# SBUF pools of a diffusion backbone exchange their places along the partition

## The chip, the cores and the metric

The kernel runs on one core of a Trainium2 chip. The metric is the device time in microseconds of one execution; the number quoted for a kernel is the median of its runs. The profile is of one more execution, taken by the hardware profiler.

## The reference

A backbone of two layers over 512 latent tokens of width 1024 with 256 context tokens in front (batch 1), in float32. Layer 0 mixes with attention (4 differential heads and 8 grouped-query heads), layer 1 with a spatial-gating MLP. Each layer ends with a gated ConvFFN of inner width 2816, and all sub-layers have an adaLN-modulated RMSNorm ahead and a gated residual behind. Cut to what matters here:

```python
for l in range(DEPTH):                       # DEPTH = 2
    h_lat = modulate(rms_norm(x, mix_norm[l]), sh1, sc1)
    y_lat = attention_mixer(...) if l % 2 == 0 else sgu_mixer(...)
    x = x + g1 * y_lat
    x = x + g2 * conv_ffn(modulate(rms_norm(x, ffn_norm[l]), sh2, sc2), ...)
return rms_norm(x, final_norm)

def conv_ffn(h, w_up, conv_w, conv_b, w_down):
    z = h @ w_up                              # 1024 -> 5632
    z = conv_w[0] * z[t-1] + conv_w[1] * z[t] + conv_w[2] * z[t+1] + conv_b
    g, u = jnp.split(z, 2, axis=-1)
    return (jax.nn.silu(g) * u) @ w_down      # 2816 -> 1024
```

## The kernel before

The weights are cut into 182 units of 128x1024 float32 (`N_UNITS`, line 50). `fetch` (line 185) loads a unit by a DMA of SP's queue into one of four `raws` buffers. `ens` (line 286) then splits it into a high part (a cast on ACT, line 292) and a low part (a subtraction on DVE, line 296, through `sub`, line 137), both of type fp32r, each in a tile of its own. A product of two split operands is three matmuls, high by high, high by low, low by high (`mm3`, line 131), so a unit, which holds eight 128x128 blocks, stands for 24 matmuls, each with its own weight load.

The FFN is `ffn` (line 1051). Up projection: 44 units a layer, each one 128-row block of the output; units 0 to 3 run as two halves of 256 columns, where the norm of the tokens is still being finished, and units 4 to 43 with all 512 columns. Down projection (`out_proj`, line 961): 8 output blocks m of 22 k-steps each, so k-step q = 22 m + k takes block q % 8 of unit q // 8, 22 units a layer; m = 0 to 5 with 512 columns, m = 6 and 7 as halves of 256. In both, the weights are the stationary operand; the activations, the moving operand, lie in slots.

Where a split unit goes is decided by `wslot` (line 278). The two FFNs' units go in part to the weight pool `wpool` (`area2`, six tiles of 4 KiB a partition), the rest to `slots` (37 such tiles):

```python
for b, n, per in ((U_UP0, 44, 4), (U_DN0, 22, 8), (U_UP1, 44, 4), (U_DN1, 22, 8)):
    if b <= u < b + n and (u - b) % per < 3:
        return area2.tile([128, 1024], F32R, name=nm(p), tag="W2")
return slot(p)
```

So of four up units the first three lie in the weight pool and the fourth in slots; of eight down units the first three in the weight pool and five in slots. A pool unit has two of the six tiles (high and low), and three units go once round the pool.

The pools stand one behind the other in each partition, in the order in which they are opened (lines 76 to 81). In the compiled program, counted in KiB from the start of the partition: 16 reserved by the compiler and a few constants of its own; `const` to 23.5; `slots` 23.5 to 171.5; `raws` 171.5 to 187.5; `temps` (six buffers of 2 KiB) to 199.5; `tiny` to 199.9; then `att`, eight buffers of 3 KiB for the score tiles of attention and a few tables, 199.9 to 223.9. After attention `att` is closed (line 940) and `wpool`, 24 KiB as well, is opened in the same place (line 943). In each down projection the tiles of its unit 0 start at 199.9 and 219.9, those of unit 1 at 215.9 and 211.9, those of unit 2 at 207.9 and 203.9. The compiler places tiles up to 224 KiB.

In attention, a score tile (`e`, line 651) lies in `att`; `ptrans` (line 657) transposes it 128x128 at a time on TensorE with the score block as the stationary operand and `ident` as the moving one (`tr`, line 128); `build_q` (line 608) does the same with blocks of q from slots. `ones_m` is the stationary operand of the norm sums (`rstd_bc`, line 311), whose moving operand is in temps. `row_mm` (line 352) multiplies the adaLN matrices of layer 0, read from raws as moving operands (tiles `am`).

Of the kernel before, what the change touches and what calls it, by code (L numbers as in the profile page):

```python
# [9 lines left out]
F32 = mybir.dt.float32  # L10
# [43 lines left out]
def hybrid_backbone(  # L54
# [18 lines left out]
    nc = tc.nc  # L73
    V, A, G, T_, SY = nc.vector, nc.scalar, nc.gpsimd, nc.tensor, nc.sync

    const = ctx.enter_context(tc.tile_pool(name="const", bufs=1))
    slots = ctx.enter_context(tc.tile_pool(name="slots", bufs=37))
    raws = ctx.enter_context(tc.tile_pool(name="raws", bufs=4))
    temps = ctx.enter_context(tc.tile_pool(name="temps", bufs=6))
    tiny = ctx.enter_context(tc.tile_pool(name="tiny", bufs=12))  # L80
    area = tc.tile_pool(name="att", bufs=8)
    att = area.__enter__()
    psP = ctx.enter_context(tc.tile_pool(name="psP", bufs=4, space=PSUM))
# [60 lines left out]
    sm = const.tile([128, SM_COLS], F32, name="sm")  # L144
    cw = const.tile([128, 352], F32, name="cw")
    cb = const.tile([128, D], F32, name="cb")
    ident = const.tile([128, 128], F32, name="ident")
    ones_m = const.tile([128, 128], F32, name="ones_m")
    md = const.tile([128, 96], F32, name="md")
    tab1 = att.tile([128, 768], F32, name="tab1", tag="E")  # L150
    tab2 = att.tile([128, 768], F32, name="tab2", tag="E")
# [1170 lines left out]
```

## Time and profile before

| | us |
|---|---|
| median of 3 runs (1290.22 to 1291.27) | 1290.73 |
| the profiled execution | 1293.27 |
| its span, first to last instruction | 1291.5 |
| TensorE busy | 1239.1 (96%) |
| VectorE busy | 757.9 (59%) |
| ScalarE busy | 594.4 (46%) |
| GpSimd busy | 248.1 (19%) |
| the four longest unbroken TensorE pieces of the chain | 709.7 |

Engines are PE (TensorE matmul), PEld (its weight loads), DVE (VectorE), ACT (ScalarE), POOL (GpSimd), SP (SyncE, which issues DMAs). L126 is a line of the kernel; nearly all matmuls stand under L126, the line of `mm`, so they are told apart by what they write: `up` and `op` are the up and down projections, `sc` scores, `pt` transposed scores. Matmuls overlap, so a matmul's own duration is longer than the time from one to the next; that time is had by dividing a stretch by the weight loads that start in it (the x behind PEld).

### The profile page before, as it was taken

To read this page: it belongs to the slowest core of one execution; us is meant where nothing else is said; L and a number is where in the kernel's file an instruction comes from. 1 tells how busy PE (TensorE), PEld (TensorE's weight loads), DVE (VectorE), ACT (ScalarE), POOL (GpSimd) and SP (SyncE) were. 2 spreads that over 40 slices of the span, in tenths; PEclk is the share of its full clock that TensorE was granted. 3 is DMA by queue.
4 is the path that set the end of the run, shared out by engine and by line. 5 is a ranking of instruction groups with operands and counts; after the bars stand their busy time and mean duration, and the time that the engine had idled before them with its cause. 6 is when DMAs were issued, how large, how long until landed. Compare 5 with 4: busy or idle time off the path is not lost.

```text
span 1291.5 us, 17180 instructions
## 1 busy us (share of the span) xinstructions
PE 1239.1 (96%) x6722; PEld 1043.7 (81%) x6722; DVE 757.9 (59%) x1116; ACT 594.4 (46%) x970; POOL 248.1 (19%) x171
## 2 busy tenths in 40 slices
PE   5899999889989999999999999999999999999997
PEld 3688988777769888888888898888988888888887
DVE  4466367688867866666775433455575565655312
ACT  3343355676645665666543134433454444444211
POOL 0102266564540344444600000000000000000001
PEclk9999999999889999999999999999999999999999
DMA  9521434763321455555577404224033232325201
GB/s 371 201 66 37 128 115 147 216 176 99 98 82 34 151 192 196 194 195 179 166 258 246 148 3 145 82 82 147 19 128 99 83 113 82 102 94 163 82 1 66
DMA packets 49505, 167.40 MB, mean 130 GB/s; under 512 B 6144, under 2 KB 6672, under 8 KB 49424
## 3 DMA queue, kind: packets, MB, share of 16 engines
q1 hardware_dynamic: 49424, 166.30, 39.3%
q8 instruction: 53, 0.87, 0.3%
q14 instruction: 28, 0.23, 0.1%
HBM read 152.12 MB, written 2.10 MB: 119 GB/s over the span
## 4 chain that ended last, share of the span: by engine, by line
PE 74%; DVE 3%; ACT 1%; POOL 0%; DMA 0%; issue 0%; DVEq 0%; SPq 0%; ACTq 0%; POOLq 0%
PE up L126 38%; PE op L126 23%; PE su L126 3%; PE sv L126 3%; PE sc L126 1%; PE og L126 1%; PE po L126 1%; DVE osq L758 1%; PE pt L129 1%; PE mx L126 1%; PE pn L126 1%; PE nps L126 1%; DVE mx L650 1%; DVE u L331 0%; DMA kk<-ks 0%
## 5 line engine op out<-in xcount | busy, mean ns | idle before, releaser
L126 PE MATMUL up<-h,wh 128*128 128x512 f32 (+1 forms) x1536 | 447.0, 375 | 0.7 <-DVE h L333 0.6
L126 PEld LDWEIGHTS up<-h,wh 128*128 128x128 f32 x1536 | 280.4, 188 | 57.0 <-DVE h L333 1.0
L137 DVE TENSOR_TENSOR wl<-wr,wh 128x1024 fp32r<-128x1024 f32 x176 | 224.2, 1283 | 166.5 <-ACT wh L292 144.2
L126 PE MATMUL up<-h,wl 128*128 128x512 f32 (+1 forms) x768 | 286.2, 375 | 0.0
L292 ACT CAST wh<-wr 128x1024 fp32r<-128x1024 f32 x182 | 188.4, 1048 | 122.3 <-PE up L126 48.0
L126 PE MATMUL op<-p,wh 128*128 128x512 f32 (+1 forms) x880 | 227.5, 348 | 0.0
L126 PEld LDWEIGHTS op<-p,wh 128*128 128x128 f32 x880 | 154.0, 189 | 22.0
L126 PEld LDWEIGHTS up<-h,wl 128*128 128x128 f32 x768 | 144.6, 188 | 27.5
L126 PE MATMUL op<-p,wl 128*128 128x512 f32 (+1 forms) x440 | 153.0, 348 | 0.0
L252 POOL TENSOR_TENSOR ar<-ar,cb 128x1024 f32<-128x1024 f32 x40 | 98.8, 2485 | 155.9 <-DMA ar<-in_adaT_dram 110.3
L1210 POOL TENSOR_TENSOR of<-of,rstd 128x512 f32<-128x512 f32 x2 | 3.6, 1797 | 641.2 <-ACT rstd L318 641.2
L1063 DVE SCALAR_TENSOR_TENSOR z<-up,cw,z 128x511 f32<-128x511 f32 x88 | 65.4, 745 | 52.3 <-ACT z L1062 52.3
L126 PEld LDWEIGHTS op<-p,wl 128*128 128x128 f32 x440 | 83.1, 189 | 10.9
L1062 ACT ACTIVATE z<-up,cw 128x512 f32<-128x512 f32 x88 | 68.0, 774 | 21.2 <-PE up L126 21.2
L953 DVE SCALAR_TENSOR_TENSOR x<-op,md,x 128x512 f32<-128x512 f32 (+1 forms) x42 | 25.9, 622 | 87.8 <-PE op L126 87.7
L650 DVE TENSOR_REDUCE mx<-sc 128x1 f32<-128x768 f32 x64 | 60.8, 951 | 22.7 <-PE sc L126 14.7
L652 ACT ACTIVATE e<-sc,mx 128x768 f32<-128x768 f32 x64 | 57.9, 905 | 32.5 <-DVE mx L650 30.0
L1065 DVE SCALAR_TENSOR_TENSOR z<-up,cw,z 128x511 f32<-128x511 f32 x88 | 65.7, 749 | 2.7
L1068 ACT ACTIVATE z<-z 128x512 f32<-128x512 f32 x44 | 27.8, 632 | 84.7 <-DVE z L1065 84.7
L126 PE MATMUL sc<-kk,qs 128*128 128x512 f32 (+1 forms) x256 | 58.3, 349 | 7.2 <-DMA kk<-ks 6.5
L326 ACT ACTIVATE sq<-x 128x512 f32<-128x512 f32 (+1 forms) x37 | 20.4, 559 | 84.8 <-DVE x L953 84.2
L142 ACT CAST p<-z 128x512 fp32r<-128x512 f32 x44 | 27.3, 619 | 69.3 <-DVE z L1069 69.3
(206 smaller groups left out, 1879.5 us busy)
## 6 DMA issues: line engine op xcount, KB each, us to landing
wr<-in_W_dram SPq DMA_DIRECT2D x182, 512.0 KB, 3.8
ar<-in_adaT_dram SPq DMA_DIRECT2D x56, 512.0 KB, 4.5
am<-in_adaM_dram SPq DMA_DIRECT2D x24, 512.0 KB, 3.9
ar<-in_adaN_dram SPq DMA_DIRECT2D x16, 512.0 KB, 8.6
kk<-ks SPq DMA_DIRECT2D x20, 256.0 KB, 4.2
x<-in_xT_dram SPq DMA_DIRECT2D x8, 512.0 KB, 5.2
kk<-ks SPq DMA_DIRECT2D x20, 128.0 KB, 3.3
qs<-qh SPq DMA_DIRECT2D x16, 128.0 KB, 2.4
```

The costliest lines, as they stand in the source:

```text
L126: pe(T_.matmul(out=o, lhsT=l, rhs=r, start=st, stop=sp))
L137: return V.tensor_tensor(out=o, in0=a, in1=b, op=ALU.subtract)
L142: return A.copy(out=hi, in_=src), sub(lo, src, f(hi))
L252: return (G.tensor_tensor(out=tl, in0=tl, in1=cv, op=ALU.mult), A.activation(out=temp("aj", 1024, BF16), in_=tl, func=AF.Identity, accum_o ...
L292: last["hi"] = A.copy(out=hi, in_=r)
L650: V.tensor_reduce(out=m, in_=ps[:, 0:768], axis=AX.X, op=ALU.max, negate=True)
L652: A.activation(out=e, in_=ps[:, 0:768], func=AF.Exp, bias=m, scale=1.0, accum_out=sm_out)
L953: last["x"] = V.scalar_tensor_tensor(out=xv, in0=ps, scalar=md[:, gcol + m:gcol + m + 1], in1=xv, op0=ALU.mult, op1=ALU.add)
L1062: A.activation(out=t, in_=p, func=AF.Identity, bias=cw[:, cv + 3:cv + 4], scale=cw[:, cv + 1:cv + 2])
L1063: V.scalar_tensor_tensor(out=t[:, 1:512], in0=p[:, 0:511], scalar=cw[:, cv:cv + 1], in1=t[:, 1:512], op0=ALU.mult, op1=ALU.add)
L1065: V.scalar_tensor_tensor(out=t[:, 0:511], in0=p[:, 1:512], scalar=cw[:, cv + 2:cv + 3], in1=t[:, 0:511], op0=ALU.mult, op1=ALU.add)
L1068: last_silu[0] = A.activation(out=z[0], in_=z[0], func=AF.Silu)
```

## The change

`const`, `raws`, `temps` and `tiny` are opened from the right, that is from the upper end of the space downward; `slots` and `att` (and with it `wpool`, which takes its place) stay on the left. `ident` and `ones_m` move from `const` to a new pool `mats` at the very beginning of the left side. Sizes, buffer counts, loops and the order in the program are as before. Added up from the sizes, in KiB: `mats` 16.1 to 17.1, `slots` 17.1 to 165.1, `att` and later `wpool` 165.1 to 189.1; from the upper end, `const` 217.6 to 224, `raws` 201.6 to 217.6, `temps` 189.6 to 201.6, `tiny` below that.

```diff
@@ -73,11 +73,12 @@
     nc = tc.nc
     V, A, G, T_, SY = nc.vector, nc.scalar, nc.gpsimd, nc.tensor, nc.sync
 
-    const = ctx.enter_context(tc.tile_pool(name="const", bufs=1))
+    const = ctx.enter_context(tc.tile_pool(name="const", bufs=1, side="right"))
+    mats = ctx.enter_context(tc.tile_pool(name="mats", bufs=1))
     slots = ctx.enter_context(tc.tile_pool(name="slots", bufs=37))
-    raws = ctx.enter_context(tc.tile_pool(name="raws", bufs=4))
-    temps = ctx.enter_context(tc.tile_pool(name="temps", bufs=6))
-    tiny = ctx.enter_context(tc.tile_pool(name="tiny", bufs=12))
+    raws = ctx.enter_context(tc.tile_pool(name="raws", bufs=4, side="right"))
+    temps = ctx.enter_context(tc.tile_pool(name="temps", bufs=6, side="right"))
+    tiny = ctx.enter_context(tc.tile_pool(name="tiny", bufs=12, side="right"))
     area = tc.tile_pool(name="att", bufs=8)
     att = area.__enter__()
     psP = ctx.enter_context(tc.tile_pool(name="psP", bufs=4, space=PSUM))
@@ -144,8 +145,8 @@
     sm = const.tile([128, SM_COLS], F32, name="sm")
     cw = const.tile([128, 352], F32, name="cw")
     cb = const.tile([128, D], F32, name="cb")
-    ident = const.tile([128, 128], F32, name="ident")
-    ones_m = const.tile([128, 128], F32, name="ones_m")
+    ident = mats.tile([128, 128], F32, name="ident")
+    ones_m = mats.tile([128, 128], F32, name="ones_m")
     md = const.tile([128, 96], F32, name="md")
     tab1 = att.tile([128, 768], F32, name="tab1", tag="E")
     tab2 = att.tile([128, 768], F32, name="tab2", tag="E")
```

## Rows read from the trace of the kernel before

**Rows 1.** Page, busy time, share of the span and instructions of each engine.

```profile
PE 1239.1 (96%) x6722; PEld 1043.7 (81%) x6722; DVE 757.9 (59%) x1116; ACT 594.4 (46%) x970; POOL 248.1 (19%) x171
```

**Rows 2.** Chain that ended last, longest pieces: start us, us, what.

```profile
404.90 243.83 PE up L126 x1140
648.73 114.38 PE op L126 x594
...
922.49 237.08 PE up L126 x1084
1159.57 114.38 PE op L126 x594
```

**Rows 3.** Windows: stretch, length, PE PEld DVE ACT POOL busy (instructions), clock, DMA, GB/s.

```profile
404.90:648.73 243.83, 243.83 (x1142) 202.21 (x1141) 164.81 (x201) 146.20 (x220) 98.84 (x40) 1.00 0.52 173
648.73:763.11 114.38, 114.38 (x596) 98.02 (x595) 54.70 (x74) 30.22 (x36) 0.00 (x0) 1.00 0.54 180
922.49:1159.57 237.08, 237.08 (x1085) 195.50 (x1085) 148.42 (x187) 107.22 (x141) 0.00 (x0) 1.00 0.30 96
1159.57:1273.95 114.38, 114.38 (x596) 98.03 (x595) 34.99 (x37) 30.89 (x43) 0.00 (x0) 1.00 0.22 69
```

**Rows 4.** Windows, second up projection: a slot unit, then three pool units.

```profile
1020.48:1025.97 5.49, 5.49 (x25) 4.50 (x24) 2.87 (x4) 2.32 (x3) 0.00 (x0) 1.00 0.25 95
1025.97:1042.71 16.75, 16.75 (x73) 13.57 (x72) 10.54 (x13) 7.09 (x10) 0.00 (x0) 1.00 0.28 95
```

**Rows 5.** Windows, second down projection: pool units, slot units, 256 columns pool, slots.

```profile
1159.41:1176.15 16.75, 16.75 (x73) 13.57 (x72) 11.32 (x12) 8.59 (x10) 0.00 (x0) 1.00 0.49 168
1176.15:1181.64 5.49, 5.49 (x25) 4.50 (x24) 1.79 (x3) 2.52 (x3) 0.00 (x0) 1.00 0.60 177
1181.64:1203.41 21.77, 21.77 (x97) 18.02 (x96) 6.32 (x6) 4.86 (x5) 0.00 (x0) 1.00 0.38 116
1250.20:1257.33 7.13, 7.13 (x61) 7.12 (x60) 1.45 (x2) 1.03 (x2) 0.00 (x0) 1.00 0.00 0
1257.33:1265.95 8.63, 8.63 (x74) 8.63 (x73) 0.91 (x2) 3.44 (x8) 0.00 (x0) 1.00 0.01 2
...
1159.41:1164.99 5.58, 5.58 (x25) 4.52 (x24) 3.50 (x5) 3.24 (x5) 0.00 (x0) 1.00 0.00 0
1164.99:1170.56 5.57, 5.57 (x25) 4.52 (x24) 4.22 (x5) 3.25 (x4) 0.00 (x0) 1.00 0.63 203
```

**Rows 6.** TensorE timeline (start us, us): four transposes of q, of scores, what follows.

```profile
325.20 0.60 PE L129 MATMUL qt<-ident,q 128*128 128x128 f32 x4
325.56 0.47 PE L126 MATMUL og<-o,wh 128*128 128x512 f32 x1
...
350.14 0.60 PE L129 MATMUL pt<-ident,e 128*128 128x128 f32 x4
350.50 0.48 PE L126 MATMUL sc<-kk,qs 128*128 128x512 f32 x1
```

**Rows 7.** Tiles wl, wh, 1030 to 1056 us: duration ns min/median/max, first, last start.

```profile
L137 DVE TENSOR_TENSOR wl<-wr,wh x6: 1224/1226/1228, 1030.9 to 1054.8; 128x1024 fp32r<-128x1024 f32 x6
L292 ACT CAST wh<-wr x6: 1046/1048/1052, 1029.8 to 1053.8; 128x1024 fp32r<-128x1024 f32 x6
```

**Rows 8.** Tile am: duration ns min/median/max, first and last start.

```profile
L355 PE MATMUL sc<-am,tab x192: 379/379/403, 167.9 to 254.8; 128*32 128x256 f32 x192
```

**Rows 9.** Window of the start; SP's weight issues (start, us); page's DMA row.

```profile
0.00:32.00 32.00, 17.19 (x95) 9.99 (x95) 13.69 (x28) 12.69 (x18) 1.74 (x7) 1.00 0.95 371
...
6.24 1.61 SPq L189 DMA_DIRECT2D wr<-in_W_dram  x2
14.31 1.45 SPq L189 DMA_DIRECT2D wr<-in_W_dram  x2
23.32 3.94 SPq L189 DMA_DIRECT2D wr<-in_W_dram  x4
...
wr<-in_W_dram SPq DMA_DIRECT2D x182, 512.0 KB, 3.8
```

## Prediction

> **What bounds the kernel now.** I read the page's busy times first: TensorE is busy 96% of the span, every other engine at most 59% [rows 1]. Then the chain that ended last: its four longest pieces are the up and down projections of the two FFNs, unbroken TensorE, 243.83 + 114.38 + 237.08 + 114.38 = 709.7 us, 55% of the span [rows 2]. In those four stretches TensorE is busy in all of the time, ACT and DVE at most 68%, the DMA engines at most 54% [rows 3]. So in 55% of the time the end moves with one number, how long TensorE takes from one matmul to the next; work of other engines moves it only if it comes so late that TensorE starts to wait.
>
> That number isn't the same everywhere, and this is what the reader should see in the next two groups. All matmuls in them are 128x128 weights on 512 columns at the same granted clock (1.00, the 2.4 GHz level), each with its own weight load, so time over loads is the pace. In the second up projection a slot unit (24 loads) is followed by three units of the weight pool (72 loads): 16.75/72 = 232.6 ns each in the weight pool [rows 4]. The second down projection does it with other weights in another order: three pool units take 16.75 us again, 232.6 ns; the five units after them lie in slots, and their last four, 96 loads in 21.77 us, take 226.8 ns [rows 5]. The first slot unit after pool units pays a remainder: 5.49/24 = 228.7 ns [rows 4, 5]. What differs between the two kinds is where the weights lie. Tag, type and shape are alike; the activations come from slots in both. Which unit is which follows from line 280. The load on the other engines doesn't explain it: the pool units take 16.75 us with DMA at 0.28 and at 0.49, and slot units stay at 226.8 beside 0.38 [rows 4, 5]. So weights read from 199.9 to 223.9 KiB of the partition cost TensorE 16.75/72 - 21.77/96 = 5.9 ns per 512-column matmul more than weights read from 23.5 to 171.5 KiB.
>
> **The change part by part.** No instruction is added or removed, and no loop, buffer count or wait; the diff exchanges addresses. The weight pool and the score tiles before it go from 199.9-223.9 to 165.1-189.1 KiB, slots down by 6.4 KiB, raws up from 171.5 to 201.6, temps by 2 KiB, the constants to the top, except ident and ones_m, the two constants that TensorE reads.
>
> (a) Weights of the FFNs, per layer. Up: units 0 to 3 run as 256-column halves, the other 40 with 512; of these 30 lie in the pool: 30 x 24 x 5.9 ns = 4.25 us. The remainder paid by ten slot units, 5.49 less 24 x 226.8 ns = 5.44, is 0.05 us each: 0.5. Down: m 0 to 5 are 132 k-steps of three matmuls; units 0-2, 8-10 and half of 16 lie in the pool, 52 steps, 156 matmuls x 5.9 = 0.92, and two remainders 0.1. Against it: at 256 columns the pool is not dearer but cheaper, 7.13/60 = 118.8 ns against 8.63/72 = 119.9 (73 loads are counted in that window, one of which belongs to the next) [rows 5]. 144 such matmuls in the up halves and 120 in the down tail lose 1.1 ns each: 0.3. Sum: 4.25 + 0.5 + 0.92 + 0.1 - 0.3 = 5.5 us a layer, 10.9 in both. All of it lies on TensorE where TensorE alone is the chain, so it goes to the end in full, as long as weights come in time. They do: a stage that runs 2.4% faster raises ACT and DVE from 0.60 and 0.68 to 0.61 and 0.69 and DMA from 0.52 to 0.53 [rows 3].
>
> (b) Score tiles. They are stationary in 288 transposes. Four transposes of a score tile take 350.50 - 350.14 = 0.36 us, four of q, from slots, 325.56 - 325.20 = 0.36 [rows 6]. I take zero. From the resolution of these rows, 0.01 us in four, the bound is 0.7 us either way.
>
> (c) Operands of ACT, DVE and GpSimd. The splits of six units in a row, four or five of which write the pool and one or two slots, take 1046 to 1052 ns on ACT and 1224 to 1228 on DVE [rows 7]: where they write doesn't show. A read from the upper end beside one from below has no row; I take zero for it too, by the nearest rows, those writes. The other end: ACT and DVE, at most 68% busy in the four stretches, could take a third longer before TensorE waits, so in them it costs nothing either way [rows 3].
>
> (d) Moving operands that go up: the 24 am tiles in raws and the sums of squares in temps. Of the first there are 192 short matmuls [rows 8], of the second some 50. None of them has been read from the slow place yet. Bounds: zero, as the activations of rows 4 and 5 are moving operands from all over the slots at one pace, or 5.9 ns on each of 242, a loss of 1.4 us. I take zero.
>
> (e) DMA into raws. The trace has no large transfer into the upper end, so there is no row for it. A landing takes 3.8 us and four raws rotate [rows 9]; I take no change, by the nearest rows, the engine writes of (c). The other end is the rival on the slow side.
>
> Sum: 1293.27 us for the profiled execution, of which 1291.5 is the span, less 10.9 is 1282.4; from the median of the runs, 2.5 us lower, 1290.73 - 10.9 = 1279.8.
>
> **A rule that speaks against it.** The rows say that the place of the weights in the partition changes the pace [rows 4, 5]. The Trainium skill, "TensorE: Matmul & The Clock Gate", section "Step-by-step: what each phase is for", says that TensorE has a read port for the streamed operand and another for the weights, that loading the next weights takes nothing from the running matmul, and that a load's time goes by its column count. By that rule the address would not enter, and the kernel would stay at 1290.7. The trace differs by 5.9 ns a matmul, and the measurement decides; the rule is rival C all the same.
>
> **The rivals.** A, the forecast: every part of the new place is as fast as the slots: 1279.8.
>
> B, the boundary lies inside the new place. Rows cover 23.5 to 171.5 KiB as fast and 199.9 to 223.9 as slow; 165.1 to 171.5 is known, 171.5 to 189.1, 73% of the pool, is not. If all of that were slow, 27% of 10.9 is left: 1287.8; with a boundary in its middle some 64% is left: 1283.8. For it: nothing in the trace says where the step is. Against a slope that grows with the address: the first unit's tiles stand at 199.9 and 219.9 KiB, near both ends of the pool, the second's at 211.9 and 215.9, and they take 5.58 and 5.57 us [rows 5]; it is a step.
>
> C, no change: the difference comes with the pool and not with its address, say from six buffers being refilled while their neighbours are read. 1290.7. Against it: slots are refilled in the same way, and in the 7.13 us in which DVE and ACT do two instructions each and no DMA runs, the pool still keeps a pace of its own, 118.8 ns for 119.9 [rows 5].
>
> D, slower: staging tiles in the upper end land more slowly. At the start the DMA engines are busy 0.95 of 32 us at 371 GB/s, and eight of the weight transfers, 8 x 0.524 MB / 371 = 11.3 us, are issued by 27.3 us [rows 9]; in the first up projection DMA is busy 0.52, so TensorE begins to wait there when landings take 1/0.52 = 1.9 times as long [rows 3]. That is the point from which it decides: at 2.0 the start loses 11.3 and the stage 0.04 x 243.8 = 9.8, against 10.9 won: 1290.7 + 21.1 - 10.9 = 1300.9. Nothing in the trace speaks for a factor of that size.
>
> **How the numbers follow.** A 0.80, B 0.09, C 0.07, D 0.04. The likeliest is A: 1279.8. Low end: (b) wins 0.7; the 192 matmuls of rows 8, whose weights come from a table in `att`, win up to 5.9 ns each, 1.1; the runs lie 0.5 to either side of their median: 1277.5. High end: the 1.4 of (d) and 0.5 give 1281.7, and over the nearer half of B, a boundary in the upper part of the new place, it reaches to 1285.5. A change of 0.2%, 2.6 us, is about what a measurement of this kernel can tell from none. A and B are faster (B's worst, 1287.8, just so): 0.89. C is the same: 0.07. D is slower: 0.04.
>
> **What would show it.** In the profile after, the windows of three pool units, 72 loads, should take 72 x 226.8 = 16.33 us in both projections, a slot unit behind them 5.44, the two down projections some 113.3 us instead of 114.4 and the up projections 4.6 to 4.8 us less each. B shows as pool units of two paces; C as 16.75 us unchanged; D as TensorE waiting for ACT casts that wait for landings longer than 3.8 us. The transposes at 0.36 us for four test (b). I would be wrong in principle if the pool units got faster and the end didn't follow, or if slots and the pool traded paces.

## The result and the profile after

| | before | after |
|---|---|---|
| median (lowest to highest of 5 runs), us | 1290.22 (1289.53 to 1291.27) | 1277.0 (1274.7 to 1279.06) |
| ratio of after to before, 95% interval | | 0.9895 [0.9879, 0.9912] |
| profiled execution, us | 1293.27 | 1278.29 |
| its span, us | 1291.5 | 1276.4 |
| start of the first FFN's longest TensorE piece, us | 404.90 | 400.60 |
| from there to the end of the span, us | 886.6 | 875.8 |

The kernel is 13.2 us faster. I had forecast 1279.8, with a range from 1277.5 to 1285.5: the sign and the main term came in, the time lies 0.5 us below the range, and the cause that I gave is wrong, as the experiments show.

The longest pieces of the chain after, in the columns of [rows 2]; after's line numbers are before's plus one:

```profile
400.60 239.22 PE up L127 x1140
639.82 113.51 PE op L127 x594
...
912.86 232.50 PE up L127 x1084
1145.36 113.51 PE op L127 x594
```

They lose 4.61, 0.87, 4.58 and 0.87 us, 10.93 in all. The up pieces leave out the first matmuls of their stage, which have 256 columns; counted from first to last matmul, the four stages lose 10.8. The windows of the same units as in [rows 4, 5], first a slot unit and three pool units of the second up projection, then three pool units, the slot units and the two 256-column stretches of the second down projection:

```profile
1009.20:1014.64 5.44, 5.44 (x26) 4.50 (x25) 3.02 (x4) 2.33 (x3) 0.00 (x0) 1.00 0.33 96
1014.64:1030.96 16.32, 16.32 (x74) 13.51 (x73) 10.38 (x13) 7.09 (x10) 0.00 (x0) 1.00 0.31 97
1145.19:1161.51 16.32, 16.32 (x73) 13.51 (x72) 11.23 (x12) 8.67 (x10) 0.00 (x0) 1.00 0.48 166
1161.51:1166.95 5.44, 5.44 (x25) 4.50 (x24) 1.87 (x3) 2.52 (x3) 0.00 (x0) 1.00 0.59 194
1166.95:1188.71 21.76, 21.76 (x97) 18.02 (x96) 6.32 (x6) 4.84 (x5) 0.00 (x0) 1.00 0.36 118
1234.95:1242.15 7.20, 7.20 (x62) 7.19 (x61) 1.44 (x2) 1.03 (x2) 0.00 (x0) 1.00 0.00 0
1242.15:1250.79 8.64, 8.64 (x75) 8.64 (x74) 0.91 (x2) 3.43 (x8) 0.00 (x0) 1.00 0.01 2
```

The stretches hold the same 24, 72, 72, 24, 96, 60 and 72 matmuls as before; where a count is one or two higher, a neighbour's start falls on the rounded edge. The pool units' pace went from 232.6 to 16.32/72 = 226.7 ns, and slots stay at 21.76/96 = 226.7. At 256 columns the pool lost its lead: 7.20/60 = 120.0 ns for 118.8, the slots' 8.64/72 = 120.0. All at a granted clock of 1.00. So the FFNs gave what the sum said, and two kinds of weights became one.

The other 4.3 us lie ahead of the first FFN. Two windows of attention, where the granted clock differs, first of before, then of after (its span is shifted by 1 to 4 us, so the work in them is only nearly the same):

```profile
313.00:318.00 5.00, 4.63 (x14) 3.17 (x15) 4.35 (x8) 1.39 (x3) 0.00 (x0) 0.69 0.05 21
336.00:346.00 10.00, 7.91 (x26) 5.62 (x27) 8.67 (x8) 5.14 (x9) 4.05 (x2) 0.66 0.30 90
```

```profile
313.00:318.00 5.00, 5.00 (x26) 3.96 (x25) 4.91 (x7) 3.52 (x7) 0.00 (x0) 1.00 0.21 49
336.00:346.00 10.00, 8.53 (x52) 6.83 (x51) 10.00 (x15) 6.36 (x12) 2.89 (x3) 1.00 0.33 107
```

Before shows the 1.2 GHz level in part of both stretches, after in neither. Whether the layout has to do with that was one of the questions for the experiments.

### The profile page after: what moved, and what is told of

The parts are those of the page before. It is cut to its first block, busy times and chain, and to the rows that moved or that the text cites. A ratio compares the mean times of both kernels' runs of the same rounds, so it can differ in the third digit from the quotient of the medians.

```text
span 1276.4 us, 17180 instructions
## 1 busy us (share of the span) xinstructions
PE 1224.5 (96%) x6722; PEld 1040.6 (82%) x6722; DVE 763.0 (60%) x1116; ACT 594.0 (47%) x970; POOL 250.8 (20%) x171
## 4 chain that ended last, share of the span: by engine, by line
PE 74%; DVE 3%; ACT 1%; POOL 0%; DMA 0%; issue 0%; DVEq 0%; SPq 0%; ACTq 0%; POOLq 0%
PE up L127 38%; PE op L127 23%; PE su L127 3%; PE sv L127 3%; PE sc L127 1%; PE po L127 1%; PE og L127 1%; DVE osq L759 1%; PE pt L130 1%; PE mx L127 1%; PE nps L127 1%; DVE mx L651 1%; DVE u L332 0%; PE pn L127 0%; DMA kk<-ks 0%
## 5 line engine op out<-in xcount | busy, mean ns | idle before, releaser
L127 PE MATMUL up<-h,wh 128*128 128x512 f32 (+1 forms) x1536 | 441.1, 372 | 0.7 <-DVE h L334 0.6
L138 DVE TENSOR_TENSOR wl<-wr,wh 128x1024 fp32r<-128x1024 f32 x176 | 227.6, 1304 | 156.3 <-ACT wh L293 133.2
L127 PE MATMUL up<-h,wl 128*128 128x512 f32 (+1 forms) x768 | 283.1, 371 | 0.0
L127 PEld LDWEIGHTS op<-p,wl 128*128 128x128 f32 x440 | 83.3, 189 | 10.2
L127 PE MATMUL gp<-wh,h 128*128 128x256 f32 (+1 forms) x256 | 59.0, 317 | 0.0
```

The source lines that it names most:

```text
L127: pe(T_.matmul(out=o, lhsT=l, rhs=r, start=st, stop=sp))
L138: return V.tensor_tensor(out=o, in0=a, in1=b, op=ALU.subtract)
```

## The experiments

Distance, below, is the address of a matmul's weights less that of its moving operand, in bytes, taken modulo 256 (or 512 where that is said), from the tiles' addresses in the compiled program. In before, slots start at byte 24,096 and the pool at 204,704, 180,608 apart: 44 x 4096 + 384. All tiles of both are 4096 bytes, all weight blocks in them 512 bytes apart. So a slot weight is always 0 from an activation, which lies in slots too, and a pool weight 384, that is 128 modulo 256. The 384 bytes are `tiny`, which stands between the two. After, `tiny` is elsewhere and every distance is 0. That is a second reading of the same rows, next to mine.

**Repeats.** The kernel before and the one after once more, without an edit.

> The kernel before, once more, for a second trace. The address theory explains 10.9 us of the change, all in the two FFNs; the two traces differ by 15.1 us, of which 4.2 us lie in attention, where the first trace of before has four stretches at a granted clock of 0.5 (20.5 us in all) and the trace of after two (10.2 us). If these stretches are chance from one execution to the next, this trace has another number of them than four, or has them elsewhere, and its attention part (130 to 377 us) is shorter or longer with that number. If they come from the place of the score tiles, this trace has the same four. The FFN stretches should be the same in any case: three pool units 16.75 us.

> The changed kernel, once more. Address theory: pool units 16.33 us for three, up and down projections as in the first trace of after, 10.9 us less than before from 377 us on. Rest of the gain (2.3 us of the medians): if it is chance in the clock, the number of stretches at 0.5 differs from the two of the first trace and the attention part goes with it; if it belongs to the change, there are two again.

1289.88 and 1277.34 us, ratios 1.0008 [0.9997, 1.002] and 0.9905 [0.9889, 0.9922]; each ratio, here and below, is to runs of before made beside it, and its interval is a 95% one. The four FFN stages repeat within 0.05 us in every trace of either kernel. What lies ahead of them doesn't: the first FFN's long piece started at 404.90 and 403.09 us in two traces of before, 400.60 and 397.63 in two of after. The stretches at a granted clock of 0.5 move as well: before has four (20.5 us in all, the first at 280 us) in one trace and five (23.9 us, the first at 20 us) in the other, after two (10.2 us) in both, at 280 and 359 us in one, at 20 and 358 us in the other. So where they fall differs between executions of one program.

**Raws alone to the upper end.** The pool moves down by 16 KiB, across the boundary of my theory; distance stays 384.

```diff
-    raws = ctx.enter_context(tc.tile_pool(name="raws", bufs=4))
+    raws = ctx.enter_context(tc.tile_pool(name="raws", bufs=4, side="right"))
```

> The kernel before with one pool moved: raws to the upper end, so that the weight pool and score tiles lie from 183.9 to 207.9 KiB. A boundary at 192 KiB: of 1752 matmuls with 512 columns whose weights lay in the slow place 1112 still do, so 37% of 10.9 = 4.0 us are won, and the pace changes from block to block inside the pool at 192.0. A boundary below 183.9: nothing is won. A boundary between 192 and 199.9: more than 4.0. The pool theory (the tiles are slow because they are a pool of six): nothing is won and all pool units keep 232.6 ns. Raws in the upper end being slow to land (rival D): slower than before, TensorE waits for weights.

1288.35 us, ratio 0.9994 [0.9982, 1.0007]. The three pool units of the second up projection and of the second down projection:

```profile
1020.94:1037.68 16.74, 16.74 (x73) 13.57 (x72) 10.53 (x13) 7.10 (x10) 0.00 (x0) 1.00 0.30 95
1154.38:1171.12 16.74, 16.74 (x73) 13.56 (x72) 11.86 (x12) 8.60 (x10) 0.00 (x0) 1.00 0.48 166
```

16.74/72 = 232.5 ns, as before, in tiles from 183.9 to 207.9 KiB. In after the tiles from 184 to 189 KiB were fast. One place, two paces: it isn't the place.

**Slots alone to the upper end.** Slots go to 76 to 224 KiB, the pool to 51.9 to 75.9; distance becomes 448 (192 modulo 256).

```diff
-    slots = ctx.enter_context(tc.tile_pool(name="slots", bufs=37))
+    slots = ctx.enter_context(tc.tile_pool(name="slots", bufs=37, side="right"))
```

> The kernel before with one pool moved: the 37 slots to the upper end (76 to 224 KiB), weight pool at 51.9 to 75.9 KiB. Eight of the slots then lie above 192 KiB and hold weights, activations, q, k and residuals as they come. In one trace all four pairings occur: weights low or high, moving operand low or high. Address of the weights alone: 465 matmuls with 512 columns have high weights, 570 a high moving operand; high weights 232.6 ns, high moving operand with low weights 226.8; 465 x 5.9 = 2.7 us are lost of the 10.9 won: 8.2 us faster than before. If the moving operand counts as well, another 3.4 us are lost: 4.8 faster. The pool theory: the pool units stay at 232.6 and nothing is won.

1279.71 us, ratio 0.9928 [0.9909, 0.9946]. Pool units, then the slot units of the down projection:

```profile
1144.67:1161.15 16.48, 16.48 (x74) 13.52 (x72) 11.62 (x12) 8.84 (x11) 0.00 (x0) 1.00 0.48 164
1166.59:1188.35 21.76, 21.76 (x98) 18.03 (x97) 6.31 (x6) 4.85 (x5) 0.00 (x0) 1.00 0.37 114
```

Now the pool is the low one and still the slower, 16.48/72 = 228.9 ns, a value that neither kernel had. Slots are at 226.7 although eight of them lie above 192 KiB, as weights and as moving operands. A third pace with a third distance: the address theory falls on both sides, and so does the theory of the pool as such, which left 232.6. The four FFN stages lose 8.7 us, near the 8.2 that the address theory gave here, so the total alone would have spoken for it; the paces decide. This kernel also rules out the other neighbours: the weights' own address (160 modulo 256) and their distances from the starts of raws, temps and tiny (128 each) are the same as in before, and only the one from slots is new.

**Tiny alone to the upper end.** The pool moves by 384 bytes, to 199.5 to 223.5 KiB, and the distance becomes 0.

```diff
-    tiny = ctx.enter_context(tc.tile_pool(name="tiny", bufs=12))
+    tiny = ctx.enter_context(tc.tile_pool(name="tiny", bufs=12, side="right"))
```

> The kernel before with one pool of 384 bytes, tiny, moved to the upper end; it had stood between the slots and the weight pool. The weight pool stays high, at 199.5 to 223.5 KiB, but its tiles now start at a whole multiple of 512 bytes from the activations' tiles in the slots instead of 384 bytes past one. Offset theory (the pace goes by the distance of weights and activations modulo 512 bytes): three pool units 16.32 us, the two FFNs 10.8 us shorter, as in the changed kernel. Address theory: nothing changes, three pool units 16.75 us.

**Tiny alone back.** The kernel after, with `tiny` left between slots and the pool: the pool is at 165.5 to 189.5 KiB, distance 384.

```diff
-    tiny = ctx.enter_context(tc.tile_pool(name="tiny", bufs=12, side="right"))
+    tiny = ctx.enter_context(tc.tile_pool(name="tiny", bufs=12))
```

> The changed kernel with tiny opened on the left again, between slots and weight pool: the pool stays below 192 KiB (165.5 to 189.5), and its tiles start 384 bytes past a multiple of 512 from the activations. Offset theory: three pool units 16.75 us as before the change, and the 10.8 us of the FFNs are lost again. Address theory with a boundary above 189.5 KiB: as fast as the changed kernel.

1278.97 us, ratio 0.9908 [0.9892, 0.9925], for tiny alone to the upper end; 1289.01, 0.9986 [0.9972, 0.9999], for tiny alone back. Up and down pieces of the first FFN, first with tiny at the upper end, then with tiny back:

```profile
400.86 239.22 PE up L126 x1140
640.08 113.51 PE op L126 x594
```

```profile
401.22 243.75 PE up L127 x1140
644.96 114.38 PE op L127 x594
```

Moving 384 bytes wins the whole FFN part with the pool left in its "slow" place, and putting them back loses it with the pool in its "fast" place. The weights' own address modulo 256 doesn't decide either: pool weights at 160 were slow in before and at 228.9 ns with slots alone at the upper end; those at 0 were slow with tiny back, those at 128 (after) and 32 (tiny at the upper end) fast. What is left is the distance from the moving operand.

**The distance, step by step.** The kernel after with 36 slots and a pool of one buffer for each of its tiles, in which a gap and paddings set the three pool units of a round at a distance each: here 64, 128 and 192 (gap 16 words, paddings 16 and 16), in the other two 256, 320, 480 (gap 64, paddings 16 and 40) and 32, 96, 160 (gap 8, paddings 16 and 16).

```diff
-                return area2.tile([128, 1024], F32R, name=nm(p), tag="W2")
+                i = (u - b) % per
+                w2 = ((0, 16), (0, 16), (0, 0))[i][p == "wl"]
+                return area2.tile([128, 1024], F32R, name=nm(p), tag=f"W{i}{p}", padded_shape=[128, 1024 + w2])
...
+    V.memset(area2.tile([128, 16], F32, name="gap", tag="gap"), 0.0)
```

> The changed kernel with 36 slots for 37 and gaps in the weight pool, so that the three units of a round stand 64, 128 and 192 bytes past a multiple of 512 from the activations; the slot units stay at 0. Offset theory: each of the three keeps a pace of its own, different from the 226.7 ns of offset 0, and repeats it at every round; by the two offsets seen so far (384: 232.4 ns, 448: 228.9 ns) the pace rises with the distance from the nearest multiple of 512, so 64 about 228.9, 128 about 232.4, 192 more. A theory of the absolute place: all three at one pace, 226.7. Its time is not of use, as it has one slot less.

> The same with offsets 256, 320 and 480. Offset theory: 256 the dearest, 320 between it and the 232.4 ns of 384, 480 below the 228.9 ns of 448. A theory of the absolute place: all at 226.7. Its time is not of use, as it has one slot less.

> The sweep once more, with offsets of 32, 96 and 160 bytes. The runs before show a period of 256 bytes: 0 and 256 at 226.7 ns, 64 and 320 at 233.3, 128 and 384 at 232.4, 192 and 448 at 228.9, 480 (224 past a multiple of 256) at 233.5. Offset theory: each of the three has a pace of its own that repeats at every round, all above 226.7; if odd multiples of 32 behave alike, 32, 96 and 160 stand near the 233.5 of 480. The theory of the absolute place: 226.7 for all. Its time is not of use, as it has one slot less.

The three pool units in a row, one line each, in the order of the distances above (64, 128, 192, then 256, 320, 480, then 32, 96, 160):

```profile
1018.32:1023.92 5.60, 5.60 (x26) 4.51 (x25) 3.57 (x5) 2.39 (x4) 0.00 (x0) 1.00 0.01 1
1023.92:1029.49 5.57, 5.57 (x25) 4.52 (x24) 3.17 (x4) 2.36 (x4) 0.00 (x0) 1.00 0.59 162
1029.49:1035.00 5.51, 5.51 (x25) 4.51 (x24) 3.70 (x5) 2.35 (x4) 0.00 (x0) 1.00 0.39 125
```

```profile
1018.78:1024.22 5.44, 5.44 (x25) 4.50 (x24) 3.41 (x5) 2.38 (x4) 0.00 (x0) 1.00 0.01 2
1024.22:1029.82 5.60, 5.60 (x26) 4.51 (x24) 3.34 (x4) 2.37 (x4) 0.00 (x0) 1.00 0.55 168
1029.82:1035.42 5.60, 5.60 (x26) 4.50 (x25) 3.80 (x5) 2.36 (x4) 0.00 (x0) 1.00 0.37 116
```

```profile
1021.41:1027.01 5.60, 5.60 (x25) 4.51 (x24) 3.57 (x5) 2.38 (x4) 0.00 (x0) 1.00 0.00 1
1027.01:1032.63 5.62, 5.62 (x26) 4.52 (x24) 3.17 (x4) 2.36 (x4) 0.00 (x0) 1.00 0.55 170
1032.63:1038.23 5.60, 5.60 (x26) 4.51 (x24) 3.80 (x5) 2.35 (x4) 0.00 (x0) 1.00 0.37 113
```

Means over all matmuls of 512 columns whose neighbours, ten in all, have the same distance (some 340 each here, some 1490 in before and with slots at the upper end); another choice of neighbours moves them by some 0.5 ns:

| distance modulo 512 | 0, 256 | 32 | 64, 320 | 96 | 128, 384 | 160 | 448, 192 | 480 |
|---|---|---|---|---|---|---|---|---|
| ns from one matmul to the next | 226.7 | 233.3 | 233.3 | 234.3 | 232.4 | 233.5 | 228.9 | 233.5 |

64 and 320 agree, as do 128 and 384, 192 and 448, and 256 is as good as 0: what counts is the distance modulo 256, 0 is the only fast one among those tried, and 192 stands in between. The order that I had expected of the first two steps, a pace that rises with the distance from a multiple of 512, was wrong: 64 is dearer than 192, and 256 is not the dearest but as fast as 0. The third came out as expected. The whole kernel follows: 1284.69, 1284.87 and 1289.24 us in one execution each.

**Zero for 512 columns, 192 for the halves.** The kernel after, 36 slots, pool tiles 4352 bytes apart; the units that run only as 256-column halves start 192 bytes into theirs. Unit 16 of each down projection, of which half runs with 512 columns, stays at 0.

```diff
-                return area2.tile([128, 1024], F32R, name=nm(p), tag="W2")
+                o = 48 if (per == 4 and u - b < 4) or (per == 8 and u - b > 16) else 0
+                return area2.tile([128, 1088], F32R, name=nm(p), tag="W2")[:, o:o + 1024]
```

> The changed kernel with 36 slots for 37 and pool tiles of 4352 bytes, in which the units that run only as halves of 256 columns (up 0 to 2, down 17 and 18 of each layer) start 192 bytes into the tile, all others at its start. At 256 columns the offset 192 (448) costs 116.7 ns a matmul and 0 costs 120.0, so 480 matmuls win 3.3 ns each: 1.6 us less in the two FFNs than the changed kernel, if one slot less costs nothing, which the sweeps' stretches outside the FFNs bear out. If the gain at 256 columns belongs to something else than the offset, the FFNs take what they take in the changed kernel.

1276.68 us, ratio 0.9895 [0.988, 0.9911]. The 60 pool matmuls of the tail, then the last 48 of them, those of the moved units 17 and 18, and the slots' behind them:

```profile
1233.79:1240.66 6.87, 6.87 (x61) 6.87 (x60) 1.44 (x2) 1.03 (x2) 0.00 (x0) 1.00 0.00 0
1235.22:1240.66 5.44, 5.44 (x50) 5.44 (x49) 0.69 (x1) 0.58 (x2) 0.00 (x0) 1.00 0.00 0
1240.66:1249.30 8.64, 8.64 (x75) 8.64 (x73) 0.91 (x2) 0.82 (x2) 0.00 (x0) 1.00 0.01 2
```

5.44/48 = 113.3 ns at distance 192, beside 120.0 at distance 0: at 256 columns 0 is not the fastest. But there the distance modulo 256 doesn't settle the pace. With slots alone at the upper end, where every pool weight is at 192, the same 60 matmuls of the tail take 7.07/60 = 117.8 ns on the first half of the columns and 6.80/60 = 113.3 on the second:

```profile
1234.77:1241.84 7.07, 7.07 (x62) 7.07 (x61) 1.44 (x2) 1.03 (x2) 0.00 (x0) 1.00 0.00 0
1250.47:1257.27 6.80, 6.80 (x63) 6.80 (x61) 0.48 (x1) 0.42 (x1) 0.00 (x0) 1.00 0.00 0
```

The four FFN stages take 2.2 us less than after's. The whole kernel, 1276.68 us, lies among the medians of after alone (1276.4 to 1277.3), so I don't call this version faster.

**After and tiny alone, side by side.** Both once more on one chip, because tiny alone had come out 2 us behind after with equal FFN stages.

> The changed kernel, beside the next one on the same chip. Offset theory: 10.8 us in the FFNs, and what the medians show beyond that (12.3 and 13.2 so far) is chance in the start and in attention, whose stretches at a granted clock of 0.5 differ from execution to execution; then this kernel and the next one have the same time. If the rest of the exchange (constants, raws, temps, score tiles, ident and ones_m) wins something of its own, this kernel is 1 to 2 us below the next.

> The kernel before with tiny alone on the right, again. Offset theory: the same time as the changed kernel beside it, within a microsecond. If the rest of the exchange wins something of its own: 1 to 2 us above it.

1276.38 us, ratio 0.9899 [0.9886, 0.9913], and 1280.43, 0.9929 [0.9916, 0.9942]. FFN pieces again equal. So some of after's gain seemed to lie elsewhere. A candidate was the alignment of slots for the DMAs that write them: their start is a multiple of 64 bytes in after, and 32 past one in before and with tiny alone.

**Slots shifted by 32 bytes.** A tile of 32 bytes ahead of `ident`, in the kernel after (shown), with tiny alone at the upper end, and in before (in these two in `const`, where `ident` lies); distances stay.

```diff
+    shift = mats.tile([128, 8], F32, name="shift")
     ident = mats.tile([128, 128], F32, name="ident")
```

> The changed kernel with 32 bytes of padding ahead of ident: slots and the weight pool now start 32 bytes past a multiple of 64 (as in the kernel before and in the one with tiny alone at the upper end), raws still at a multiple of 64, weights still a multiple of 4096 bytes from the activations. Theory alignment (the 2 to 4 us by which the changed kernel leads the one with tiny alone come from the DMA that writes slots at unaligned addresses): 1279 to 1280 us. Theory chance (the lead comes from when the half-clock stretches of attention fall): the median stays within 1276 to 1278.5. Both: up projections 242.2 and 242.0 us, down projections 122.3 and 122.2, as in the changed kernel.

> The kernel before with tiny alone at the upper end, and 32 bytes of padding ahead of ident: slots, raws and the weight pool now start at multiples of 64 bytes, everything else is left where it was. Theory alignment: 1276 to 1277.5 us, as the changed kernel. Theory chance: 1279 to 1280.5, as tiny alone gave twice. Both: FFN stretches as in the changed kernel.

> The kernel before with 32 bytes of padding ahead of ident: slots, raws and the weight pool start at multiples of 64 bytes, and the weight pool is still 384 bytes (modulo 4096) from the activations. Theory alignment: some 2 to 3 us less than before, ratio about 0.998, from the stages ahead of the first FFN. Theory chance: ratio 1.000. Both: FFN stretches 246.8, 123.2, 246.5 and 123.0 us as before, since only the distance between weights and activations counts there.

1278.51, 1277.75 and 1288.37 us; ratios 0.991 [0.9896, 0.9923], 0.9908 [0.9894, 0.9922] and 0.9995 [0.9986, 1.0004]. Only before with the shift decides: it should have won 2 to 3 us and won nothing that shows, so alignment isn't it. The first two came out between the theories, and after's lead over tiny alone (2 and 4 us in the sessions ahead) turned into 0.8 us behind it, within their intervals.

What is left ahead of the first FFN is seen from all traces together, by the start of the first long piece:

| distance | starts, us |
|---|---|
| 384 (before twice, raws, tiny back, before shifted) | 404.90, 403.09, 399.90, 401.22, 398.07 |
| 0 (after three times, tiny twice, after shifted, tiny shifted) | 400.60, 397.63, 398.13, 400.86, 403.14, 401.05, 399.11 |
| others (slots, three steps; halves) | 397.79, 399.18, 400.12, 399.33, 401.03 |

One and the same program differs by 3.0 us (after) and 2.3 us (tiny alone); the kernels of the three steps and the one with the halves have the same program up to there, but for one memset, and span 1.9 us. Over the first 395 us the granted clock goes along only in part. They are, of before, of after, and of tiny alone:

```profile
0.00:395.00 395.00, 351.32 (x2331) 295.39 (x2332) 256.95 (x465) 201.51 (x398) 145.68 (x129) 0.97 0.44 143
```

```profile
0.00:395.00 395.00, 351.73 (x2364) 297.15 (x2365) 258.88 (x470) 202.45 (x401) 145.98 (x129) 0.99 0.45 143
```

```profile
0.00:395.00 395.00, 351.94 (x2362) 297.91 (x2363) 258.98 (x470) 202.35 (x400) 145.90 (x129) 0.97 0.45 143
```

Tiny alone, at before's 0.97, is as far as after at 0.99 (2362 and 2364 matmuls started, 2331 in before). But some of these stretches lie at the start, where TensorE is idle much of the time ([rows 9]: 17.19 of 32 us busy). Between 130 and 395 us alone the starts of the table go with the clock: 404.90 at a mean of 0.96 (one trace), on average 401.5 at 0.97 (six), 399.3 at 0.98 (five) and 398.9 at 0.99 (five). Before itself has 0.96, 0.97 and, shifted, 0.98, after 0.98 and twice 0.99, tiny alone twice 0.97 and, shifted, 0.98.

Over the first 395 us all three traces of after have 0.99 and so does after shifted; tiny alone has 0.97 in both of its traces. So the layout may have some part in when the clock falls in attention, but I have no run that sets this apart from chance. It stays open, as the 1 to 3 us that it would be.

## Why the prediction was right or wrong

**Bound and pace: right.** Time over loads in the stretches where TensorE alone is the chain was the quantity that the change moved, and its gain went to the end whole: 875.8 us from the first long piece to the end instead of 886.6. In the first layer DMA rose from 0.52 and 0.54 to 0.54 and 0.56, and VectorE in the up projection from 0.68 to 0.71, where I had 0.69 (and a stage 2.4% faster, which is the pool units' gain; the stage as a whole gained 1.9%); its work was still done in time [rows 3]:

```profile
400.60:639.82 239.22, 239.22 (x1142) 201.78 (x1141) 170.22 (x201) 145.85 (x219) 101.22 (x40) 1.00 0.54 175
639.82:753.33 113.51, 113.51 (x596) 98.08 (x595) 55.05 (x75) 30.30 (x36) 0.00 (x0) 1.00 0.56 184
```

**The step that failed: "What differs between the two kinds is where the weights lie."** Tag, type and shape were alike, but one more thing differed, where the weights lie relative to the activations. In before, place and distance go together for every matmul of [rows 4, 5], so no row could part them, and I named the one as the cause without listing the other. It was to be had from the addresses that I had added up: 384 bytes of `tiny` stand between two pools whose other sizes are multiples of 4096. Sign and size held by luck, because the change happens to move `tiny` too. By my theory, tiny alone to the upper end would have done nothing and raws alone would have won a part; the chip showed the reverse: tiny alone won the 10.8 us of the four FFN stages, and raws alone 0.1, with its pool units at 232.5 ns. What sets the pace is the distance modulo 256, 232.4 ns at 128 and 226.7 at 0.

**The size of (a): right.** 10.9 against 10.8. Each down projection gave 0.87, as the terms 0.92 + 0.1 less 120 x 1.1 ns say; the "some 113.3 us" of the last part was a slip, 114.4 less those terms is 113.5, as measured. The 256-column loss came as the 1.1 to 1.2 ns of [rows 5], but not with a cause that I had named: that pool units were cheaper there goes with the distance as well. With tiny alone at the upper end they take 7.20/60 = 120.0 there too.

**(b) to (e): right in size.** Four transposes of scores take 321.82 - 321.47 = 0.35 us, where before had 0.36 [rows 6], though the distance of score tile and `ident` went from 64 to 0: to 0.01 us, these four don't show it.

```profile
321.47 0.60 PE L130 MATMUL pt<-ident,e 128*128 128x128 f32 x4
321.82 0.48 PE L127 MATMUL sc<-kk,qs 128*128 128x512 f32 x1
```

The splits stay, with either place as their target [rows 7], and so do am from the upper end and the landings of raws [rows 8, 9]:

```profile
L138 DVE TENSOR_TENSOR wl<-wr,wh x6: 1224/1225/1226, 1019.5 to 1042.9; 128x1024 fp32r<-128x1024 f32 x6
...
L293 ACT CAST wh<-wr x6: 1044/1049/1052, 1018.5 to 1041.8; 128x1024 fp32r<-128x1024 f32 x6
...
L356 PE MATMUL sc<-am,tab x192: 379/379/403, 167.2 to 254.2; 128*32 128x256 f32 x192
...
wr<-in_W_dram SPq DMA_DIRECT2D x182, 512.0 KB, 3.8
```

**The rivals.** B fell with the cause: all three pool units share one pace in after, and there is no boundary. C had the better name, the pool and not its address, but its mechanism, refilling, falls: with the same refilling the pool runs at 226.7 to 234.3 ns by the padding alone. D falls with landings of 3.8 us. The rule weighed against the change, separate read ports in the Trainium skill, "TensorE: Matmul & The Clock Gate", section "Step-by-step: what each phase is for", would have left the time at 1290.7. The runs disagree, by up to 7.6 ns a matmul, and they say more than before's trace did: what counts is a relation between the addresses of the two operands.

**The range.** The time came out 0.5 us below its low end. Of the 2.3 us that I allowed downward, 1.8 stood for (b) and (d), which gave nothing that shows, and 0.5 for runs around the median. What I put at nothing was a difference in the stages ahead of the first FFN. The FFNs' 10.8 us alone would give 1290.22 - 10.8 = 1279.4; the other 2.4 us of the medians lie ahead, where one program differs by 3 us from trace to trace, which a single trace can't show but the spread of after's own runs (4.4 us) does. Predicted from the profiled execution, 1282.4, the miss is 4.1 us, and 4.3 is what the start of the first long piece moved. The medians of the seven runs at distance 0, after and tiny alone with their repeats and shifts, lie 9.1 to 13.2 us below before's beside them, on both sides of 10.8. So the 0.5 us can't be told from chance. The 1290.73 that I started from is also above before's medians beside the experiments (1289.23 to 1290.12), by up to 1.5 us.

## What to carry to other kernels

When two kinds of the same matmul have different paces, list for both operands the address modulo small powers of two, and their difference, before the place in memory is blamed; a small pool between two large ones is enough to set it. Here 512-column fp32r matmuls were fastest with their weights a multiple of 256 bytes from the moving operand, worth 2.2 to 7.6 ns of some 230 each, while the transposes looked at showed nothing and at 256 columns that distance was the slowest. A theory that gives the right size may still have the wrong cause: one edit of one pool, 384 bytes, told the two apart.

## What the runs showed of the hardware

The pace of 512-column fp32r matmuls with a weight load each depends on the distance of the two operands' addresses modulo 256: 226.7 ns at 0, 228.9 at 192, 232.4 at 128, 233.3 to 234.3 at 32, 64, 96, 160 and 224, all at a granted clock of 1.00. At 256 columns 0 is the slowest, 120.0, and the others lie between 113.3 and 119.8, with 192 at 113.3 on one half of the columns and at 117.8 on the other of the same kernel, so the distance modulo 256 doesn't settle it there; no order that I could read. What in the chip makes the distance count was not tried. Nor can these runs tell whether it is the distance from the matmul's own moving operand or from that of the matmul that runs while the weights are loaded: both lie in slots. The Trainium skill, "TensorE: Matmul & The Clock Gate", section "Wait — 56ns, not 53.3ns?", gives 215.7 ns from one matmul to the next at 512 columns and the full clock; the best here, with a weight load for each, is 226.7.
